# RWKV steps of a hybrid block: outputs in the state's own PSUM bank, a third set of operands, U times M made ahead, and later filling

## The chip, the cores and the metric

The kernel runs on one core of one Trainium2 chip. The metric is the time of one execution on the device in microseconds (us), lower is better; the median of several runs is compared. Engines are named as in the profile: PE is TensorE (PEld its weight loads), DVE VectorE, ACT ScalarE, POOL GpSimd, SP the queue that issues the DMAs.

## The reference

Four layers work on 256 latent and 256 context tokens of width 1024. A layer normalises and modulates the tokens, projects them to 67 blocks of 128 columns, and sends these through three token mixers: gated DeltaNet (GDN, 4 heads), RWKV-7 (8 heads of 64) and mLSTM (4 heads). Every mixer runs in both directions, over the context first and then over the latents, starting from the context's final state. Their outputs are projected, gated and summed, and a mixture of 16 experts follows. In the last layer the context's outputs are not needed any more, only its final states.

```python
def rwkv7_scan(inp, S0):                 # state S (heads, 64, 64)
    def step(S, xt):
        r_t, w_t, k_t, v_t, a_t, b_t = xt
        sa = einsum('bhvk,bhk->bhv', S, a_t)
        S = S * w_t + sa[..., None] * b_t + v_t[..., None] * k_t
        return S, einsum('bhvk,bhk->bhv', S, r_t)

for l in range(DEPTH):
    gdn, rwkv, mlstm, gate = split_cols(modulate(rmsnorm(x, g1), *mod) @ w_in[l])
    a, b, m = gdn_branch(gdn), rwkv_branch(rwkv), mlstm_branch(mlstm)
    x = x + mod[2] * merge_branches((a, b, m), gate, w_branch[l], w_out[l])
    x = x + mod[5] * moe_ec(modulate(rmsnorm(x, g2), *mod), ...)
```

## The kernel before

The 512 tokens (context first) stand on the free axis, channels on the partitions. A layer (`layer`) starts with `rms_scale` and a loop over eight channel blocks that scales, modulates and splits them (`split`) into a rounded high part `hh`, written by ACT, and the rest `hl`, subtracted by POOL; both go to TensorE. `w_in(b, t, ...)` projects one block: its weights are loaded and split in the same way (`load_w`, lines 366 and 367), then 24 matmuls follow (`dense`, line 393).

The order of the work is made by a planner that places, on each engine, the ready instruction with the lowest number first; the program sets that number by due times, in units of about a microsecond from the layer's start (`at`, and `z.due`, which also lets the number grow with the matmul work issued). What is placed stays in that order on the engine; each engine's queue is then executed in order. `D_R`, `D_G` and `T_M` are the due distance of two RWKV pairs, that of two GDN heads, and the start of the mLSTM. `FILL` holds the due times of 36 projections that no scan needs soon (24 gate blocks, 4 output gates, 8 mLSTM inputs): they fill TensorE between the steps of the scans and are stored to DRAM (`gates`). `F0` and `F1` say over which part of the layer's due times they are spread.

RWKV works on pairs of heads, four per layer (`rwkv_pair`). A pair has two streams of tokens, the context (st = 0) and the latents (st = 1), each with both directions. A unit (`rwkv_units`) is one pair and stream: `rwkv_prep` makes the scaled operands AR and BK from decay and keys; `rwkv_unit` multiplies them to the triangles M1, transposes BK and the values (BKt, UV) and stores the triangles to DRAM (`tri_load`). `tri_inverse` inverts the 64x64 triangles of both units at once: small diagonal blocks by substitution on VectorE (lines 428 and 429), then products on TensorE. `rwkv_steps` walks four chunks in each direction. It first makes F, the product of M1 and the values (pf, copied at line 956). A step then multiplies the state X with AR (into bank pu, and, for the outputs, into another bank py), adds F to get R (line 988), multiplies with the inverse, copies the result into UV (lines 994 and 995), and multiplies that with BKt for the next state (lines 1017 and 1018) and with M1 for the outputs, which line 1010 or 1012 reads. After the steps the tail of the pair normalises the outputs and multiplies them by a gate made from R["sgd"] (lines 788 to 808).

PSUM has eight banks: one each for `dm` and `df` (projections) and `ad`, two `ai` (RWKV, mLSTM: `psm`), one `ac` (`psc`), two `bi` (GDN). M1, UV, BKt, AR and two small scale tiles have two buffers, BK one. After RWKV's last tail its SBUF pool is given to the mLSTM; `gdn(3)` is issued there. At the end of the mLSTM line 1448 normalises it, and the branches are merged.

Of the kernel before, what the change touches and what calls it, by code (L numbers as in the profile page):

```python
# [79 lines left out]
BLK = 11.5  # L80
CH = 2
DT = BLK / 8 * 1.0
D_R, D_G, T_M = 160.0, 210.0, 660.0
T1 = 5
P_R, P_G, P_M = D_R * 2.6 / 240, D_G * 3.5 / 170, 8.0
SH = 0.0
# [8 lines left out]


FILL = _fill()
F0, F1 = 0.0, 1.0
SVB = 1
PL = 1  # L100
OFF, PS = 0.0, 1.0
# [52 lines left out]
def tile_backbone(ctx: ExitStack, tc: tile.TileContext, A, out, dbg=None, depth=DEPTH):  # L154
# [319 lines left out]
    def layer(l, P, last, ahead):  # L474
# [14 lines left out]
        gates = dp.tile([40, 128, 512], F32, tag="gates", name=nm("gates"))  # L489
        part = dp.tile([8, 128, 512], F32, tag="part", name=nm("part"))  # L490

        def gated(i, db, ab, th, f):
# [42 lines left out]
                    sy.dma_start(dbg["mg"][:, db, :], acc)  # L535
            return mh, ml

        with scope("gdn", "bi", "bi", 3) as zg:
            with scope("rwkv", "ai", "ac", 3) as zr:

                xT = X["sb"]
                r = rms_scale(zr, X["ss"], 0, "sgd")
                if l > 0:
                    X["dram"] = dp.tile([128, 8, 512], F32, tag="xd", name=nm("xd"))
                    sy.dma_start(X["dram"], xT)
# [1 line left out]
                for k in range(8):  # L547
                    t = zr.mt([512], "t2")
                    ve.tensor_tensor(t, xT[:, k, :], r, ALU.mult)
                    for s in range(2):  # L550
                        ts_ = t[:, s * 256:(s + 1) * 256]
                        ve.tensor_scalar(ts_, ts_, der[:, 0, k, s:s + 1], mod[:, k, s:s + 1], ALU.mult, ALU.add)
                    split(hh[:, k, :], hl[:, k, :], t, gp)

                clock["base"] = tc.cur_priority + 100000

# [13 lines left out]

                at(0)
                G = small_gates(zg, l, P, hh, hl)
                R = rwkv_begin(zr, l, P, w_in, oc)
                pair = [rwkv_inputs(zr, l, 0, P, R, w_in, oc)]
                S = {}

# [129 lines left out]
        return G  # L706


    def rwkv_begin(z, l, P, w_in, oc):
# [23 lines left out]
        thw, adm, sgd = z.mt([512], "thw"), z.mt([512], "adm"), z.mt([512], "sgd")  # L733
        ps = w_in(B_RW, 0)
        shift_mix(ps, 12, thw)
        se.activation(thw, thw, AF.Tanh)
        ps = w_in(B_RA, 0)
        shift_mix(ps, 13, adm)
        ps = w_in(B_RG, 0, oc)
        shift_mix(ps, 14, sgd, oc)  # L740
        se.activation(sgd[:, oc:], sgd[:, oc:], AF.Tanh, scale=0.5)
        ve.tensor_scalar(sgd[:, oc:], sgd[:, oc:], 0.5, 0.5, ALU.mult, ALU.add)
        hb = z.mt([4, 8], "hb")
        ve.tensor_scalar(hb[:, 0, :], P["w0"], 0.5, None, ALU.mult)
        ve.tensor_scalar(hb[:, 1, :], P["a0"], 0.5, None, ALU.mult)
# [3 lines left out]
        return dict(shift_mix=shift_mix, thw=thw, adm=adm, sgd=sgd, hb=hb, ws=ws)  # L749

    def rwkv_inputs(z, l, b, P, R, w_in, oc):

# [11 lines left out]
    def rwkv_units(z, l, b, P, R, pair, units, last, oc, sts=(0, 1)):  # L764

        for st in sts:
            noy = last and st == 0
            z.due(D_R * (b - (0.3, 0.15)[st]), P_R * PS)
            units[b, st] = rwkv_unit(z, b, st, pair[b]["vb"], noy, rwkv_prep(z, b, st, P, R, pair[b], noy, oc))

    def rwkv_pair(z, l, b, P, R, pair, units, dst, last, oc):
# [4 lines left out]
        z.due(D_R * b, P_R * PS)  # L776
        un = [units.pop((b, st)) for st in range(2)]
        inv = tri_inverse(z, 2, lambda g, p, q: un[g]["M1"][64 * p:64 * p + 64, p, q // 4, q % 4, 0:64])
        S = None
        for st in range(2):  # L780
            z.due(D_R * (b + 0.5 + 0.25 * st), P_R * PS)
            S = rwkv_steps(z, st, un[st], inv[st], Y, S, last and st == 0)
            if b < 3 and st == 0:
                rwkv_units(z, l, b + 1, P, R, pair, units, last, oc, (0,))
        z.due(D_R * (b + 1), P_R * PS)

        n = slice(oc, 512)
# [27 lines left out]

    def rwkv_prep(z, b, st, P, R, pr, noy, oc):
# [18 lines left out]
        scl = z.mt([2, 4], "scl", 2)  # L835
        er0 = z.mt([2], "er0", 2)

        def c4(t):
            return t.rearrange("p (c w) -> p c w", c=4)
# [103 lines left out]
    def rwkv_steps(z, st, un, inv, Y, S, noy):  # L943
# [4 lines left out]

        def c4(t):
            return t.rearrange("p (c w) -> p c w", c=4)  # L950
        pf = z.psm()
        for q in range(8):
            for p in range(2):
                hp, vp = slice(64 * p, 64 * p + 64), slice(64 - 64 * p, 128 - 64 * p)
                z.mm(pf[hp, q * 64:q * 64 + 64], M1[vp, p, q // 4, q % 4, 0:64], UV[vp, q // 4, q % 4, p, :], start=True, stop=True)
        ve.tensor_copy(F, pf.rearrange("q (s w) -> q s w", s=8))
        Fv = F.rearrange("p (d s) w -> p d s w", d=2)

        X = None
# [1 line left out]
            X = z.mt([2, 64], "X", 3)  # L961
            ve.tensor_tensor(X, S, er0[:, :, None].to_broadcast([128, 2, 64]), ALU.mult)
        for s in range(4):
            pu = z.psc()
            rhs = Fv[:, :, s, :]
            if X is not None:
                for d in range(2):
                    for p in range(2):
                        hp = slice(64 * p, 64 * p + 64)
                        z.mm(pu[hp, d * 64:d * 64 + 64], AR[hp, d, ch(d, s), 0, :], X[hp, d, :], start=True, stop=True)  # L970


            lo_first = s < 2
            po = None
            if not noy:
                py = z.psm()

                def po(d, hp):
                    sl = d if lo_first else 1 - d
                    return py[hp, sl * 64:sl * 64 + 64]  # L980
                if X is not None:
                    for d in range(2):
                        for p in range(2):
                            hp = slice(64 * p, 64 * p + 64)
                            z.mm(po(d, hp), X[hp, d, :], AR[hp, d, ch(d, s), 1, :], start=d == 0, stop=False, skip_group_check=True)
            if X is not None:
                rhs = z.mt([2, 64], "R", 2)
                ve.tensor_tensor(rhs, pu[:, 0:128].rearrange("p (d w) -> p d w", d=2), Fv[:, :, s, :], ALU.add)
            for d in range(2):
                for p in range(2):  # L990
                    hp = slice(64 * p, 64 * p + 64)
                    z.mm(pu[hp, 256 + d * 64:320 + d * 64], U[hp, d * 4 + s, :], rhs[hp, d, :], start=True, stop=True)
            puv = pu[:, 256:384].rearrange("p (d w) -> p d w", d=2)
            ve.tensor_copy(UV[0:64, :, s, 0, :], puv[0:64])
            ve.tensor_copy(UV[64:128, :, s, 1, :], puv[64:128])
            for d in range(2):
                q = d * 4 + s
                for p in range(2):
                    hp = slice(64 * p, 64 * p + 64)
                    z.mm(pu[hp, 128 + d * 64:192 + d * 64], BKt[:, q, 64 * p:64 * p + 64], UV[:, d, s, p, :], start=True, stop=True)  # L1000
            if not noy:
                for d in range(2):
                    for p in range(2):
                        hp = slice(64 * p, 64 * p + 64)
                        z.mm(po(d, hp), UV[:, d, s, p, :], M1[:, p, d, s, 64:128], start=X is None and d == 0, stop=True, skip_group_check=True)
                a, e = min(s, 3 - s), max(s, 3 - s)
                yv = c4(Y[:, tk])[:, a::(e - a), :][:, 0:2, :]
                pyv = py[:, 0:128].rearrange("p (d w) -> p d w", d=2)
# [752 lines left out]
```

## Time and profile before

| | |
|---|---|
| median of 3 runs | 5061.66 us (5058.88 to 5065.56) |
| the profiled execution's own time | 5072.66 us |
| its span | 5070.9 us |
| mean granted TensorE clock | 0.937 of full speed |
| busy: PE, PEld, DVE | 4530.9, 2946.4, 3067.7 us |
| busy: ACT, POOL | 1417.9, 1432.1 us |

The span reaches from the first to the last instruction; the execution's own time is 1.8 us more. Busy time of PE is modelled, since matmuls are pipelined, and the clock counts beside it. The second layer, from which most rows come, runs from about 1330 to 2620: its first stretch to 1460, the middle to 2114, the end of the scans to 2240, the merge to 2340, and the experts.

### The profile page before, as it was taken

How to read it: one execution, taken by the hardware profiler on the slowest of the kernel's cores; microseconds unless marked ns; L12 is line 12 of the kernel's file. 1: busy time of each engine (PE TensorE's matmuls, PEld its weight loads, DVE VectorE, ACT ScalarE, POOL GpSimd, SP SyncE). 2: the span in 40 equal slices, each digit the busy share in tenths (PEclk: the TensorE clock that was granted, in tenths of full speed). 3: DMA queues.
4: the chain of work that ended last, by engine and by line, in shares of the span. 5: the costliest groups of instructions: out<-in, count | busy, mean ns of one | idle time of the engine just before them, and what ended most of it. 6: DMA issues, size and time to landing. Idle time of an engine off the chain costs nothing. (4 is left out here: it accounts for less than half of the span.)

```text
span 5070.9 us, 84827 instructions
## 1 busy us (share of the span) xinstructions
PE 4530.9 (89%) x31882; PEld 2946.4 (58%) x31882; DVE 3067.7 (60%) x8291; ACT 1417.9 (28%) x2748; POOL 1432.1 (28%) x1831
## 2 busy tenths in 40 slices
PE   7999999899899989889989998998998898887698
PEld 4666666653366666666336666665633666765533
DVE  4777666733477786573337777657433778766422
ACT  3332322220243333222014333322311433321211
POOL 3332332320243242223014334222300534431400
PEclk9999998899999999989999999997999999887899
DMA  5444444579632434346973243443698223322598
GB/s 187 133 125 138 129 143 155 180 264 394 235 109 79 135 99 139 110 157 252 393 271 114 85 125 101 128 115 129 229 387 306 84 84 92 95 77 77 194 389 316
DMA packets 681131, 881.45 MB, mean 174 GB/s; under 512 B 336752, under 2 KB 360304, under 8 KB 667920
## 3 DMA queue, kind: packets, MB, share of 16 engines
q1 hardware_dynamic: 680720, 876.02, 51.5%
q8 instruction: 252, 4.13, 0.3%
q14 instruction: 159, 1.30, 0.1%
HBM read 792.14 MB, written 83.71 MB: 173 GB/s over the span
## 5 line engine op out<-in xcount | busy, mean ns | idle before, releaser
L367 POOL TENSOR_TENSOR wlo<-wraw,whi 128x512 fp32r<-128x512 f32 x696 | 943.5, 1360 | 1969.4 <-ACT whi L366 1806.5
L393 PE MATMUL df<-big,whi 128*128 128x512 f32 (+1 forms) x2944 | 897.0, 385 | 1.7 <-POOL big L367 1.7
L393 PE MATMUL dm<-big,whi 128*128 128x512 f32 (+1 forms) x2368 | 732.1, 388 | 0.0
L366 ACT CAST whi<-wraw 128x512 fp32r<-128x512 f32 x696 | 426.0, 617 | 1045.4 <-PE df L393 528.3
L393 PE MATMUL df<-big,wlo 128*128 128x512 f32 (+1 forms) x1536 | 648.3, 422 | 54.8 <-ACT gt L565 13.5
L393 PEld LDWEIGHTS df<-big,whi 128*128 128x128 f32 x2944 | 564.2, 200 | 97.0 <-issue 6.5
L393 PE MATMUL dm<-big,wlo 128*128 128x512 f32 (+1 forms) x1248 | 521.2, 418 | 46.9 <-POOL wlo L367 13.4
L393 PEld LDWEIGHTS dm<-big,whi 128*128 128x128 f32 x2368 | 453.9, 196 | 80.6 <-issue 1.6
L393 PEld LDWEIGHTS df<-big,wlo 128*128 128x128 f32 x1536 | 304.1, 198 | 187.8 <-issue 86.2
L393 PEld LDWEIGHTS dm<-big,wlo 128*128 128x128 f32 x1248 | 244.7, 196 | 136.8 <-issue 49.9
L1647 PE MATMUL df<-mw,big 128*64 128x512 f32 x1024 | 302.2, 610 | 0.0
L1034 DVE SCALAR_TENSOR_TENSOR cv<-cv,par,cv 128x189 f32<-128x189 f32 (+3 forms) x472 | 243.2, 527 | 38.3 <-ACT cv L1031 33.8
L1694 DVE SCALAR_TENSOR_TENSOR big<-bi,der,big 128x256 f32<-128x256 f32 x448 | 191.8, 479 | 119.7 <-PE bi L1691 119.3
L1647 PE MATMUL dm<-mw,big 128*64 128x512 f32 x1024 | 255.6, 594 | 2.2 <-DMA mw<-in_w_dram 2.1
L1654 POOL MEMSET mada<- 128x512 f32 x32 | 16.8, 524 | 799.8 <-PE bi L1691 350.4
L722 DVE SCALAR_TENSOR_TENSOR big<-cv,muc,big 128x255 f32<-128x255 f32 (+2 forms) x280 | 158.1, 587 | 27.1 <-ACT big L719 24.8
L1647 PEld LDWEIGHTS dm<-mw,big 128*64 128x64 f32 x1024 | 80.8, 137 | 152.4 <-issue 137.0
L211 PE MATMUL ai<-AR,BK 64*128 64x128 f32 (+1 forms) x1024 | 104.6, 311 | 62.0 <-DVE BK L895 32.2
L1685 DVE SCALAR_TENSOR_TENSOR mlof<-ac,aff,mhif 128x512 fp32r<-128x512 f32 x32 | 24.0, 750 | 212.3 <-ACT mhif L1684 212.3
L1681 PE MATMUL ac<-mw,mrawf 128*64 128x512 f32 x512 | 139.6, 600 | 9.9 <-ACT mrawf L1675 9.9
L211 PEld LDWEIGHTS ai<-AR,BK 64*128 64x128 f32 x1024 | 85.9, 207 | 96.0 <-issue 33.2
L308 PE MATMUL ad<-adaw,cs 128*32 128x512 f32 x768 | 116.5, 659 | 26.2 <-DMA adaw<-in_ada_w_dram 21.4
(515 smaller groups left out, 7938.0 us busy)
## 6 DMA issues: line engine op xcount, KB each, us to landing
mw<-in_w_dram SPq DMA_DIRECT2D x768, 512.0 KB, 10.2
wraw<-in_w_in_dram SPq DMA_DIRECT2D x536, 256.0 KB, 2.8
adaw<-in_ada_w_dram SPq DMA_DIRECT2D x96, 1024.0 KB, 5.9
gates<-gt SPq DMA_DIRECT2D x114, 256.0 KB, 3.1
wraw<-in_w_branch_dram SPq DMA_DIRECT2D x96, 256.0 KB, 2.9
t<-gates SPq DMA_DIRECT2D x73, 256.0 KB, 3.5
TU<-zoai SPq DMA_DIRECT2D x128, 128.0 KB, 3.4
wraw<-in_w_out_dram SPq DMA_DIRECT2D x64, 256.0 KB, 5.4
```

Of the source, the lines that this page charges most:

```text
L211: mm(o, a, b, **kw)
L308: mm(ps[32 * j:32 * j + 32, :], cs[:, k, :], wt[:, j, :], start=(k == 0), stop=(k == 7), tile_position=(0, 32 * j))
L366: se.copy(dst_hi, src)
L367: eng.tensor_tensor(dst_lo, src, dst_hi.bitcast(F32), ALU.subtract)
L393: mm(ps[:, c0:c1], a[:, k % 4, :], bk[:, c0:c1], start=(n == 0), stop=(n == 3 * nk - 1))
L722: ve.scalar_tensor_tensor(dst, src, muc[:, 1 + q, rb:rb + 1], dst, ALU.mult, ALU.add)
L1034: ve.scalar_tensor_tensor(dst, src, cw[:, cb, t:t + 1], dst, ALU.mult, ALU.add)
L1647: mm(ps[64 * q:64 * q + 64, :], xe[k // 4][:, k % 4, e0 + q, :], wt[q][:, k2 * 512:(k2 + 1) * 512], start=(k == 0), stop=(k == 7))
L1654: gp.memset(Ow, 0.0)
L1681: mm(py[hf][64 * q:64 * q + 64, :], hT[:, kk, 64 * q:64 * q + 64], wt[q][:, hf * 512:(hf + 1) * 512], start=(kk == 0), stop=(kk == 3))
L1685: ve.scalar_tensor_tensor(yl[hf], py[hf], aff, yh[hf].bitcast(F32), ALU.mult, ALU.subtract)
L1694: ve.scalar_tensor_tensor(xT[:, db, cs_], pcb[:, cs_], der[:, 3, db, s:s + 1], xT[:, db, cs_], ALU.mult, ALU.add)
```

## The change

Eight edits, all within the mixers of a layer:

- A step's outputs lie in columns 384 to 511 of the bank pu (`ac`) that also holds its other three results, in place of a bank of `ai`. Only the first matmul into each half of the partitions starts the bank. The X products for the outputs are issued before R is added. The copy of the upper half of UV, and the output read of the first two steps, go from VectorE to ScalarE.
- AR and the two scale tiles have three buffers.
- F is made for both streams right behind the inverse, in place of at the head of each stream's steps.
- The second unit of the next pair is issued ahead of the pair's tail, and is due 0.1 of a pair earlier, as the first is. The steps are due at 0.4 and 0.55 of a pair in place of 0.5 and 0.75.
- The gate input `sgd` is stored to DRAM and loaded by each tail; its SBUF tile goes. `rms_scale` uses another tile.
- GDN has two scratch buffers `t2` in place of three.
- D_G is 195 for 210, T_M 650 for 660, and the filling is due from 0.1 of the time on.
- The split of hh and hl alternates between POOL and VectorE.

```diff
-D_R, D_G, T_M = 160.0, 210.0, 660.0
+D_R, D_G, T_M = 160.0, 195.0, 650.0
-F0, F1 = 0.0, 1.0
+F0, F1 = 0.1, 1.0
...
-        with scope("gdn", "bi", "bi", 3) as zg:
+        with scope("gdn", "bi", "bi", 2) as zg:
-                r = rms_scale(zr, X["ss"], 0, "sgd")
+                r = rms_scale(zr, X["ss"], 0, "adm")
-                    split(hh[:, k, :], hl[:, k, :], t, gp)
+                    split(hh[:, k, :], hl[:, k, :], t, (gp, ve)[k % 2])
...
+        sy.dma_start(sgdd[:, oc:], sgd[:, oc:])
...
-            z.due(D_R * (b - (0.3, 0.15)[st]), P_R * PS)
+            z.due(D_R * (b - (0.4, 0.25)[st]), P_R * PS)
...
         inv = tri_inverse(z, 2, ...)
+        for (F, _, _), u in zip(inv, un):
+            pf = z.psm()
+            for q in range(8):
+                for p in range(2):
+                    ...
+                    z.mm(pf[hp, q * 64:q * 64 + 64], u["M1"][vp, p, q // 4, q % 4, 0:64], u["UV"][vp, q // 4, q % 4, p, :], start=True, stop=True)
+            ve.tensor_copy(F, pf.rearrange("q (s w) -> q s w", s=8))
         for st in range(2):
-            z.due(D_R * (b + 0.5 + 0.25 * st), P_R * PS)
+            z.due(D_R * (b + 0.4 + 0.15 * st), P_R * PS)
             S = rwkv_steps(z, st, un[st], inv[st], Y, S, last and st == 0)
             if b < 3 and st == 0:
                 rwkv_units(z, l, b + 1, P, R, pair, units, last, oc, (0,))
+        if b < 3:
+            rwkv_units(z, l, b + 1, P, R, pair, units, last, oc, (1,))
         z.due(D_R * (b + 1), P_R * PS)
...
-        z.mm(pgt[:, n], gup, R["sgd"][:, n], start=True, stop=True)
         av = z.mt([512], "t2")
+        sy.dma_start(av[:, n], R["sgd"][:, n])
+        z.mm(pgt[:, n], gup, av[:, n], start=True, stop=True)
...
-        if b < 3:
-            rwkv_units(z, l, b + 1, P, R, pair, units, last, oc, (1,))
...
-        AR, BK = z.mt([2, 4, 2, 64], "AR", 2), z.mt([2, 4, 2, 64], "BK")
+        AR, BK = z.mt([2, 4, 2, 64], "AR", 3), z.mt([2, 4, 2, 64], "BK")
...
+            def mm1(o, p, a, b):
+                z.mm(o, a, b, start=p not in begun, stop=True, skip_group_check=True)
+                begun.add(p)
...
+            def po(d, hp):
+                sl = d if lo_first else 1 - d
+                return pu[hp, 384 + sl * 64:448 + sl * 64]
...
             ve.tensor_copy(UV[0:64, :, s, 0, :], puv[0:64])
-            ve.tensor_copy(UV[64:128, :, s, 1, :], puv[64:128])
+            se.copy(UV[64:128, :, s, 1, :], puv[64:128])
...
                 if lo_first:
-                    ve.tensor_copy(yv, pyv)
+                    se.copy(yv, pyv)
                 else:
                     ve.tensor_tensor(yv, yv, pyv, ALU.add)
```

## Rows read from the trace of the kernel before

**Rows 1.** Windows: span, busy time of each engine (instructions), PEclk, DMA share, GB/s.
```profile
1460.00:2114.00 654.00, 605.47 (x5519) 434.87 (x5517) 460.46 (x1317) 209.30 (x414) 210.23 (x318) 0.96 0.38 111
2114.00:2240.00 126.00, 101.68 (x534) 72.87 (x534) 94.67 (x301) 30.56 (x61) 26.91 (x29) 0.77 0.42 135
840.00:955.00 115.00, 95.83 (x460) 69.16 (x461) 88.84 (x274) 28.09 (x56) 23.61 (x23) 0.74 0.39 128
3404.00:3530.00 126.00, 101.47 (x536) 72.85 (x537) 95.60 (x302) 30.60 (x60) 27.30 (x29) 0.78 0.40 134
4030.00:4605.00 575.00, 489.63 (x5003) 394.33 (x5002) 425.67 (x1233) 190.19 (x399) 211.41 (x320) 0.90 0.31 83
4605.00:4705.00 100.00, 75.31 (x425) 55.00 (x426) 69.44 (x229) 19.47 (x46) 18.20 (x24) 0.67 0.33 97
```

**Rows 2.** Single lines from 1990 to 2260 us: durations, first and last start, forms.
```profile
L808 DVE TENSOR_TENSOR t<-ai,t x1: 678/678/678, 2116.4 to 2116.4; 128x512 f32<-128x512 f32 x1
L1220 DVE TENSOR_TENSOR Ds<-TU x8: 274/286/289, 2017.3 to 2172.7; 64x128 f32<-64x128 f32 x8
L1448 DVE TENSOR_TENSOR mH<-mH,mrr x4: 684/685/694, 2232.0 to 2233.9; 128x512 f32<-128x512 f32 x4
```

**Rows 3.** Line 565, the filling blocks' read, from 2030 to 2130 us.
```profile
L565 ACT ACTIVATE gt<-df x7: 578/590/604, 2039.9 to 2124.4; 128x512 f32<-128x512 f32 x7
```

**Rows 4.** Timeline of the second layer's second RWKV pair: start, duration, instruction.
```profile
1685.22 1.27 SPq L404 DMA_DIRECT2D ziai<-M  x2
...
1764.63 0.28 DVE L1018 TENSOR_TENSOR X<-X,scl 128x128 f32<-128x128 f32 x1
...
1787.81 0.69 DVE L956 COPY TU<-ai 128x512 f32<-128x512 f32 x1 [0.28 <-PE ai L211]
...
1808.80 0.28 DVE L1018 TENSOR_TENSOR X<-X,scl 128x128 f32<-128x128 f32 x1
...
1823.21 0.68 DVE L808 TENSOR_TENSOR t<-ai,t 128x512 f32<-128x512 f32 x1
...
1835.48 0.19 ACT L863 ACTIVATE er<-t 128x4 f32<-128x4 f32 x1
...
1847.55 1.29 SPq L404 DMA_DIRECT2D ziai<-M  x2
```

**Rows 5.** Timeline of one step of that pair, and line 995 from 1330 to 2250.
```profile
1757.34 0.40 PE L211 MATMUL ai<-M,UV 128*64 128x64 f32 x8
1757.56 0.29 DVE L1017 TENSOR_TENSOR X<-ac,X 128x128 f32<-128x128 f32 x1 [1.00 <-PE ac L211]
...
1757.80 0.29 DVE L1012 TENSOR_TENSOR big<-big,ai 128x128 f32<-128x128 f32 x1
...
1758.00 1.30 DVE L1018 TENSOR_TENSOR X<-X,scl 128x128 f32<-128x128 f32 x1
...
1759.93 0.40 PE L211 MATMUL ai<-AR,X 64*64 64x64 f32 x8
1760.14 0.29 DVE L988 TENSOR_TENSOR R<-ac,TU 128x128 f32<-128x128 f32 x1 [0.33 <-PE ac L211]
...
L995 DVE COPY UV<-ac x32: 294/295/296, 1530.9 to 2102.1; 64x128 f32<-64x128 f32 x32
```

**Rows 6.** Timeline of a unit's value copies, both out of one PSUM bank.
```profile
1690.12 0.42 DVE L938 COPY UV<-ai 64x256 f32<-64x256 f32 x1
1690.57 0.37 ACT L937 COPY UV<-ai 64x256 f32<-64x256 f32 x1 [0.98 <-DVE UV L938]
1691.17 0.41 DVE L938 COPY UV<-ai 64x256 f32<-64x256 f32 x1
```

**Rows 7.** Groups of the layer's first split: busy us, mean ns, idle before, releasers.
```profile
L367 POOL TENSOR_TENSOR big<-t,big 128x512 fp32r<-128x512 f32 x8 | 11.6, 1464 | 12.0 <-ACT big L366 12.0
...
L549 DVE TENSOR_TENSOR t<-big,sgd 128x512 f32<-128x512 f32 x8 | 8.6, 1083 | 5.1 <-POOL big L367 3.5 <-ACT sgd L362 1.6
```

**Rows 8.** Waits of ACT from 1460 to 2114 us: total, times, longest.
```profile
ACT whi L366 <- PE df L393: 119.1, 36, 9.0
```

More of the change, by code (lines that the diff above doesn't have):

```diff
@@ L488, in layer @@
         spill = [dp.tile([128, 4, 512], F32, tag=f"br{i}", name=nm("br")) for i in range(2)]
-        gates = dp.tile([40, 128, 512], F32, tag="gates", name=nm("gates"))
+        gates = dp.tile([41, 128, 512], F32, tag="gates", name=nm("gates"))
         part = dp.tile([8, 128, 512], F32, tag="part", name=nm("part"))
@@ L572, in layer @@
                 G = small_gates(zg, l, P, hh, hl)
-                R = rwkv_begin(zr, l, P, w_in, oc)
+                R = rwkv_begin(zr, l, P, w_in, oc, gates[40])
                 pair = [rwkv_inputs(zr, l, 0, P, R, w_in, oc)]
@@ L706, in small_gates, with rwkv_begin @@
         return G
-    def rwkv_begin(z, l, P, w_in, oc):
+    def rwkv_begin(z, l, P, w_in, oc, sgdd):
         muc = z.mt([5, 15], "muc")
@@ L731, in shift_mix @@
             tap(3, o[:, 256:448], p[:, 320:512])
-        thw, adm, sgd = z.mt([512], "thw"), z.mt([512], "adm"), z.mt([512], "sgd")
+        thw, adm, sgd = z.mt([512], "thw"), z.mt([512], "adm"), z.mt([512], "t2")
         ps = w_in(B_RW, 0)
@@ L748, in rwkv_begin @@
         ws = big()
-        return dict(shift_mix=shift_mix, thw=thw, adm=adm, sgd=sgd, hb=hb, ws=ws)
+        return dict(shift_mix=shift_mix, thw=thw, adm=adm, sgd=sgdd, hb=hb, ws=ws)
     def rwkv_inputs(z, l, b, P, R, w_in, oc):
@@ L778, in rwkv_pair @@
         inv = tri_inverse(z, 2, lambda g, p, q: un[g]["M1"][64 * p:64 * p + 64, p, q // 4, q % 4, 0:64])
+        for (F, _, _), u in zip(inv, un):
+            pf = z.psm()
+            for q in range(8):
+                for p in range(2):
+                    hp, vp = slice(64 * p, 64 * p + 64), slice(64 - 64 * p, 128 - 64 * p)
+                    z.mm(pf[hp, q * 64:q * 64 + 64], u["M1"][vp, p, q // 4, q % 4, 0:64], u["UV"][vp, q // 4, q % 4, p, :], start=True, stop=True)
+            ve.tensor_copy(F, pf.rearrange("q (s w) -> q s w", s=8))
         S = None
         for st in range(2):
-            z.due(D_R * (b + 0.5 + 0.25 * st), P_R * PS)
+            z.due(D_R * (b + 0.4 + 0.15 * st), P_R * PS)
             S = rwkv_steps(z, st, un[st], inv[st], Y, S, last and st == 0)
@@ L833, in rwkv_prep @@
         tk = slice(t0, t0 + 256)
-        AR, BK = z.mt([2, 4, 2, 64], "AR", 2), z.mt([2, 4, 2, 64], "BK")
-        scl = z.mt([2, 4], "scl", 2)
-        er0 = z.mt([2], "er0", 2)
+        AR, BK = z.mt([2, 4, 2, 64], "AR", 3), z.mt([2, 4, 2, 64], "BK")
+        scl = z.mt([2, 4], "scl", 3)
+        er0 = z.mt([2], "er0", 3)
         def c4(t):
@@ L950, in c4 @@
             return t.rearrange("p (c w) -> p c w", c=4)
[L951 to L956, printed above, removed]
         Fv = F.rearrange("p (d s) w -> p d s w", d=2)
@@ L963, in rwkv_steps @@
         for s in range(4):
-            pu = z.psc()
+            pu, begun = z.psc(), set()
+            def mm1(o, p, a, b):
+                z.mm(o, a, b, start=p not in begun, stop=True, skip_group_check=True)
+                begun.add(p)
+            lo_first = s < 2
+            def po(d, hp):
+                sl = d if lo_first else 1 - d
+                return pu[hp, 384 + sl * 64:448 + sl * 64]
             rhs = Fv[:, :, s, :]
@@ L969, in rwkv_steps @@
                         hp = slice(64 * p, 64 * p + 64)
[L970 to L981, printed above, removed]
+                        mm1(pu[hp, d * 64:d * 64 + 64], p, AR[hp, d, ch(d, s), 0, :], X[hp, d, :])
+                if not noy:
                     for d in range(2):
@@ L984, in rwkv_steps @@
                             hp = slice(64 * p, 64 * p + 64)
-                            z.mm(po(d, hp), X[hp, d, :], AR[hp, d, ch(d, s), 1, :], start=d == 0, stop=False, skip_group_check=True)
-            if X is not None:
+                            mm1(po(d, hp), p, X[hp, d, :], AR[hp, d, ch(d, s), 1, :])
                 rhs = z.mt([2, 64], "R", 2)
@@ L991, in rwkv_steps @@
                     hp = slice(64 * p, 64 * p + 64)
-                    z.mm(pu[hp, 256 + d * 64:320 + d * 64], U[hp, d * 4 + s, :], rhs[hp, d, :], start=True, stop=True)
+                    mm1(pu[hp, 256 + d * 64:320 + d * 64], p, U[hp, d * 4 + s, :], rhs[hp, d, :])
             puv = pu[:, 256:384].rearrange("p (d w) -> p d w", d=2)
             ve.tensor_copy(UV[0:64, :, s, 0, :], puv[0:64])
-            ve.tensor_copy(UV[64:128, :, s, 1, :], puv[64:128])
+            se.copy(UV[64:128, :, s, 1, :], puv[64:128])
             for d in range(2):
@@ L999, in rwkv_steps @@
                     hp = slice(64 * p, 64 * p + 64)
-                    z.mm(pu[hp, 128 + d * 64:192 + d * 64], BKt[:, q, 64 * p:64 * p + 64], UV[:, d, s, p, :], start=True, stop=True)
+                    mm1(pu[hp, 128 + d * 64:192 + d * 64], p, BKt[:, q, 64 * p:64 * p + 64], UV[:, d, s, p, :])
             if not noy:
@@ L1004, in rwkv_steps @@
                         hp = slice(64 * p, 64 * p + 64)
-                        z.mm(po(d, hp), UV[:, d, s, p, :], M1[:, p, d, s, 64:128], start=X is None and d == 0, stop=True, skip_group_check=True)
+                        mm1(po(d, hp), p, UV[:, d, s, p, :], M1[:, p, d, s, 64:128])
                 a, e = min(s, 3 - s), max(s, 3 - s)
                 yv = c4(Y[:, tk])[:, a::(e - a), :][:, 0:2, :]
-                pyv = py[:, 0:128].rearrange("p (d w) -> p d w", d=2)
+                pyv = pu[:, 384:512].rearrange("p (d w) -> p d w", d=2)
                 if lo_first:
-                    ve.tensor_copy(yv, pyv)
+                    se.copy(yv, pyv)
                 else:
```

## The prediction

> **What bounds the kernel now.** I read the windows by stage first, then the ends of the three scans, then one RWKV pair and one step in the timeline. The reader should look at one thing in the windows: TensorE does not run equally well everywhere. Multiply its busy time by the granted clock and one has its work in full-clock microseconds. In the second layer's long middle stretch that is 605.47 x 0.96 / 654 = 0.889 of the span; in the 126 us before the branches are merged it is 101.68 x 0.77 / 126 = 0.62, the clock having fallen to between its two levels of 1.2 and 2.4 GHz while the engine was less busy. The same dip stands at the same place in the other layers, and the last layer, with half the filling, is thin throughout (489.63 x 0.90 / 575 = 0.766) [rows 1].
>
> What runs in that dip is shown by the ends of the scans. RWKV's last output is multiplied at 2116.4, the mLSTM follows it (its tiles take RWKV's place in SBUF) and is normalised from 2232.0, and GDN's last state product is at 2172.7 [rows 2]. So the layer ends RWKV, then mLSTM, and the mLSTM waits on VectorE step by step while little else is left for TensorE: the last seven of the 36 filling blocks of this layer come out between 2039.9 and 2124.4 [rows 3]. Blocks whose due times lie 28 apart come out about 14 apart there, (2124.4 - 2039.9) / 6, so a due time is a priority and not a gate.
>
> If each dip ran at the middle stretch's rate, its work would take 95.83 x 0.74 / 0.889 = 80 us of 115 (first layer), 88 of 126 (second), 101.47 x 0.78 / 0.889 = 89 of 126 (third), and by the last layer's own rate 75.31 x 0.67 / 0.766 = 66 of 100: 35 + 38 + 37 + 34 = 144 us in four layers. From 2232.0 to 2240 only the mLSTM's own end is left, which nothing can cover; I take these 8 us off in each layer. That leaves 112 us, and it needs the mLSTM to be done about 30 us earlier in each layer.
>
> **Does the change bring the chain 30 us forward?** One RWKV pair, from the store of its triangles to that of the next, takes 162 us (1685.2 to 1847.6) [rows 4]. The first stream's last state is ready at 1764.9 but the second stream's U-times-M product is copied only by 1788.5: the next pair's first unit, due at 0.7 of a pair, went ahead of the second stream, due at 0.75. The new due times (0.6 against 0.55) and the product made ahead turn that round; up to 23.6 us. The pair's own tail, 14.8 us (to 1823.9), stands before the next pair's second unit; moving the unit ahead of it takes the tail off this path. The unit's preparation, 11.8 us to its last exponential at 1835.7, can run during the steps with a third set of operands; its products and the store, another 11.9 us, cannot, since they need the two-deep triangles and the transposed operands that the steps hold. Together up to 50 us per pair, three times per layer. The low bound is zero: the prepared work is not gone, VectorE is busy 460.46 of 654 us, and it may stretch the steps by what it used to take between them. Ten us per pair are enough; nearest to the rows, with about 30% of VectorE free, I take half, 25.
>
> The product itself, 16 matmuls and a copy per stream, is moved and stays as dear. It now stands in front of the first step for both streams, so the first stream now waits for the second's as well: a copy of 0.69 us [rows 4] and sixteen products, at four (eight instructions) in 0.40 us [rows 5] 1.6 us, so 2.3 us, which I count inside the half that I take.
>
> **What a step pays.** All its results now share one bank. In the step shown the state add (1757.56) began before the output products ended (1757.34 + 0.40), and the R add (1760.14) before the X products (1759.93 + 0.40) [rows 5]. If accesses to a bank are put in order, R waits 0.19 us more, and the state add 0.18 and then the output read. Where VectorE does that read, the products' end, the read and the add (1757.74 + 0.29 + 0.29) put the scaling at 1758.32 in place of 1758.00: 0.32 us. Where ScalarE does it, the hand-over counts: VectorE and ScalarE reading one bank took turns, from 1690.54 to 1690.57 and from 1690.94 to 1691.17, so 0.03 and 0.23 us [rows 6], and the add moves from 1757.56 to 1757.74 + 0.03 + 0.29 + 0.23 = 1758.29: up to 0.73. The second of the two UV copies, 0.295 us [rows 5], runs beside the first and is saved, or, if it too takes its turn, costs 0.23. A step therefore pays from 0.19 + 0.32 - 0.30 = 0.2 to 0.19 + 0.73 + 0.23 = 1.2 us, 2 to 9 us in the eight steps of a pair. I take 5; the chain has that to spare, so nothing enters the sum. That VectorE and ScalarE took turns in rows 6 was on the same 64 partitions. The Trainium skill, "PSUM — Partial Sum Buffer", section "PSUM bank collisions raise a hardware error", asks that two engines never touch one bank in the same 32 partitions at once, reads included, and lets different groups of 32 go together. By it the two UV copies, on opposite halves, need no turn, but the ScalarE output read, on all partitions, does: it speaks against putting the outputs there, and by it the price is 0.19 + 0.73 - 0.30 = 0.6 us in the early steps; the sum would be the same.
>
> **The first split.** GpSimd subtracts eight times, 11.6 us, and VectorE waits 3.5 us for it [rows 7]. Four go to VectorE, where a pass over 512 columns took 0.69 us (the copy in rows 4), 2.8 us. The gain is between 3.5 - 2.8 = 0.7 and half of GpSimd's 11.6, 5.8 us; I take 3 per layer, 12 in all.
>
> **Parts at nothing.** Filling due 100 later: TensorE's total is the same, and by rows 3 a free engine takes a block before its time; RWKV's first inputs go ahead of the first blocks, which I count as nothing for want of a row. GDN's earlier due times and its two instead of three scratch buffers: GDN's last product is 59 us before the normalisation, 2232.0 - 2172.7 [rows 2], and a scratch buffer more to wait for costs a store's landing per head. Storing the gate input and loading it four times per layer goes through SP's queue; the load stands in the pair's tail, no longer on the path, except after the last pair, where it may add a few us ahead of the mLSTM; that comes out of the 25. What would be queued behind a late load are SP's weight loads.
>
> **The sum.** 5072.66 - 112 - 12 = 4949 us for an execution like the profiled one. The median of the runs is 11 us under it, so 4938: I say 4940. Its own range, if only half or half as much again of the dips is won, is 4880 to 5000.
>
> **Rivals.** *GDN becomes the end.* The compressed RWKV takes its turns on VectorE. If GDN ends 30 to 40 us later, its 59 us are nearly used, and I give 10 us per layer: 5072.66 - 40 - 12 - 11 = 5010. For it: VectorE's 70%. Against it: GDN's own due times move forward. Chance 0.13.
>
> *TensorE is not the bound even in the middle.* Then the chain sets everything, up to where GDN ends: four times 59 us, 236, and 12: 5072.66 - 236 - 12 - 11 = 4814. For it: weight loads fill only 434.87 of 654 us there [rows 1]. Against it: matmuls are busy 605.47. Chance 0.07. The Trainium skill, "Perfetto Trace Analysis", section "Identifying the Most-Contended Engine", says that matmul busy time is a poor measure of how near TensorE is to its limit and names the share of weight loads; by that rule this rival would be the likeliest.
>
> *ScalarE holds up the steps: slower.* It executes in order, and two copies now stand in its queue on the state's path, twelve instructions per pair. Its casts of weights waited 119.1 us for matmuls, 36 times, 3.3 us each and 9.0 at worst [rows 8]. If each of the twelve stands 4.2 us behind such a cast, the pair's 50 us are gone, and with 9 us for hand-overs a pair is 9 longer; three pairs in four layers are 108, less the 12 of the split: 5062 + 96 = 5158. It decides from about (50 - 9) / 12 = 3.4 us each. Against it: a cast ahead of the copy can only wait for a matmul that TensorE does before it, and between steps that is a few matmuls. Chance 0.12.
>
> *It does nothing.* The order is made from due times; the chain may shorten and the other work spread into the hole: 5062, chance 0.06.
>
> **Chances and range.** The forecast has 0.62; 0.2% (10 us) is about what a measurement of this kernel can tell from no change. Faster: 0.62 + 0.13 + 0.07 = 0.82; same 0.06; slower 0.12. From 4850 to 5040 the range takes in the forecast, the GDN case and a little of the case beyond: about 0.78 together, with the GDN case's upper part at the edge.
>
> **What would show it.** The distance between two stores of RWKV triangles falls from 162 to 120-150 us; RWKV's last output comes 50 us or more earlier within its layer; the stretch before the merge has a clock above 0.9; the first GpSimd subtractions are four. A step takes up to 1 us longer from one state to the next. Wrong: the mLSTM starts as late as before; or it starts earlier and the dip only moves; or ScalarE's UV copy starts some us after its products.

## The result and the profile after

The changed kernel takes 4999.8 us in the median of four runs (4980.37 to 5006.14); the kernel before, beside it, 5063.61 (5058.88 to 5079.16). The medians lie 64 us apart; the comparison of the runs gives a ratio of 0.9848 (95% interval 0.9826 to 0.9871), which is 77 us of 5063.61. Below, versions are compared by such ratios. The forecast was 124 us, with 4999.8 inside its range, though nearer to the 5010 of the rival "GDN becomes the end" than to 4940. The profiled execution took 5006.14 us, with a span of 5004.4 and a mean granted clock of 0.948 (0.937 before).

Windows of the second layer of the changed kernel: from 100 us into the layer to the mLSTM's start, from there to its normalisation, from there to the mixture of experts.

```profile
1424.10:2047.20 623.10, 581.62 (x5389) 416.38 (x5386) 439.40 (x1293) 213.94 (x448) 196.76 (x311) 0.96 0.38 111
2047.20:2157.70 110.50, 100.62 (x574) 73.53 (x572) 87.05 (x264) 32.01 (x63) 30.88 (x30) 0.94 0.38 123
2157.70:2301.90 144.20, 131.23 (x590) 98.66 (x590) 61.02 (x103) 38.03 (x66) 60.66 (x47) 0.99 0.70 237
```

The dip is nearly gone: in the second row TensorE's work at full clock is 100.62 x 0.94 / 110.5 = 0.86 of the span, where [rows 1] gave 0.62 at a clock of 0.77. The last layer's dip is not, see below. But the third stretch, the merge, is now 144.2 us long; before it was 114.7 (880.4 to 995.1 after the layer's start). Its density is 131.23 x 0.99 / 144.2 = 0.90, so it is long because it holds more work. Single lines of the same layer show which.

```profile
L819 DVE TENSOR_TENSOR t<-ai,t x1: 692/692/692, 2035.3 to 2035.3; 128x512 f32<-128x512 f32 x1
L1223 DVE TENSOR_TENSOR Ds<-TU x8: 274/289/994, 1955.0 to 2095.5; 64x128 f32<-64x128 f32 x8
L1451 DVE TENSOR_TENSOR mH<-mH,mrr x4: 680/680/1702, 2157.7 to 2160.5; 128x512 f32<-128x512 f32 x4
L565 ACT ACTIVATE gt<-df x17: 577/592/602, 1942.4 to 2157.4; 128x512 f32<-128x512 f32 x17
L497 DVE SCALAR_TENSOR_TENSOR mg<-mg,df x8: 687/689/689, 2164.8 to 2193.2; 128x512 f32<-128x512 f32 x8
```

Counted from the first scaling of its tokens (line 549), this layer starts at 1324.1, that of before at 1351.6 ("about 1330" above was rough). Against [rows 2], RWKV's last output is at 711.2 after the layer's start in place of 764.8, GDN's last one at 771.4 in place of 821.1, and the normalisation at 833.6 in place of 880.4: 47 to 54 us earlier. GDN still ends 62 us ahead of the normalisation, so it has not become the end. The filling, which ended at 772.8 [rows 3], now ends at 833.3, so it covers the mLSTM. The eight blocks of RWKV's projected branch (the last line), which before stood in the dip, from 796.3 to 857.3 after the layer's start, now come behind the mLSTM, from 840.7 to 869.1. Of 47 us at the normalisation 17 are left where the mixture of experts begins (977.8 against 995.1).

Timeline of the second pair and its steps.

```profile
1621.38 1.26 SPq L404 DMA_DIRECT2D ziai<-M  x2
...
1687.56 0.69 DVE L786 COPY TU<-ai 128x512 f32<-128x512 f32 x1 [0.24 <-PE ai L211]
...
1689.17 0.27 DVE L997 COPY UV<-ac 64x128 f32<-64x128 f32 x1
1689.48 0.26 ACT L998 COPY UV<-ac 64x128 f32<-64x128 f32 x1 [10.34 <-DVE UV L997]
...
1691.70 0.27 ACT L1013 COPY big<-ac 128x128 f32<-128x128 f32 x1 [1.96 <-PE ac L211]
...
1691.99 0.29 DVE L1023 TENSOR_TENSOR X<-ac,scl 128x128 f32<-128x128 f32 x1 [1.81 <-ACT big L1013]
...
1694.85 0.28 DVE L997 COPY UV<-ac 64x128 f32<-64x128 f32 x1 [0.75 <-PE ac L211]
...
1695.18 0.26 ACT L998 COPY UV<-ac 64x128 f32<-64x128 f32 x1
...
1729.74 1.38 SPq L404 DMA_DIRECT2D ziai<-M  x2
...
1758.73 1.35 SPq L404 DMA_DIRECT2D ziai<-M  x2
```

From store to store this pair takes 137 us in place of 162 [rows 4]; the pairs before and after it went from 217 to 187 and from 157 to 152. The next pair's first unit is stored in mid-pair (1729.74). A step, however, is longer: from one state to the next inside a stream 7.7 us in the median of this layer's 24 distances against 5.9. The state's scaling at 1691.99 starts 0.02 us behind ScalarE's output read, and ScalarE's UV copy 0.05 us behind VectorE's.

The first split of the second layer, single lines:

```profile
L549 DVE TENSOR_TENSOR t<-big,adm x8: 684/689/693, 1324.1 to 1337.2; 128x512 f32<-128x512 f32 x8
...
L367 POOL TENSOR_TENSOR big<-t,big x4: 1297/1650/1666, 1326.7 to 1340.9; 128x512 fp32r<-128x512 f32 x4
L367 DVE TENSOR_TENSOR big<-t,big x4: 684/962/1771, 1329.0 to 1341.5; 128x512 fp32r<-128x512 f32 x4
```

Four subtractions each, as forecast. They did not get cheap: VectorE's took up to 1771 ns, and GpSimd's mean over its four is 1566 ns against 1464 over eight [rows 7].

### The profile page after: what moved, and what is told of

The parts are those of the page before. It is cut to its first block, busy times and chain, and to the rows that moved or that the text cites. A ratio compares the mean times of both kernels' runs of the same rounds, so it can differ in the third digit from the quotient of the medians.

```text
span 5004.4 us, 84862 instructions
## 1 busy us (share of the span) xinstructions
PE 4513.4 (90%) x31882; PEld 2934.2 (59%) x31882; DVE 2998.8 (60%) x8123; ACT 1470.0 (29%) x2932; POOL 1405.1 (28%) x1815
## 4 chain that ended last, share of the span: by engine, by line
PE 50%; DVE 20%; DMA 6%; issue 4%; ACT 3%; POOL 2%; SPq 0%; DVEq 0%; ACTq 0%; POOLq 0%
PE df L393 9%; PE dm L393 8%; PE df L1650 5%; PE ai L211 5%; PE bi L211 5%; PE dm L1650 4%; PE bi L1694 3%; PE ac L211 2%; PE ac L1684 2%; PE bi L1684 2%; DMA t<-gates 2%; DVE cv L1037 2%; DMA mw<-in_w_dram 1%; DVE sv L428 1%; POOL wlo L367 1%
## 5 line engine op out<-in xcount | busy, mean ns | idle before, releaser
L1037 DVE SCALAR_TENSOR_TENSOR cv<-cv,par,cv 128x255 f32<-128x255 f32 (+3 forms) x472 | 249.0, 539 | 42.6 <-ACT cv L1034 38.8
L722 DVE SCALAR_TENSOR_TENSOR big<-cv,muc,big 128x252 f32<-128x252 f32 (+2 forms) x280 | 156.6, 581 | 33.2 <-ACT big L719 31.8
L211 PE MATMUL ai<-AR,BK 64*128 64x128 f32 (+1 forms) x1024 | 124.0, 320 | 29.8 <-POOL BK L905 12.3
L1694 PEld LDWEIGHTS bi<-mada,mhif 128*128 128x128 f32 x256 | 48.0, 187 | 155.1 <-issue 82.7
L1684 PE MATMUL bi<-mw,mrawf 128*64 128x512 f32 x512 | 138.1, 592 | 0.0
```

The costliest lines, as they stand in the source:

```text
L211: mm(o, a, b, **kw)
L1037: ve.scalar_tensor_tensor(dst, src, cw[:, cb, t:t + 1], dst, ALU.mult, ALU.add)
L1684: mm(py[hf][64 * q:64 * q + 64, :], hT[:, kk, 64 * q:64 * q + 64], wt[q][:, hf * 512:(hf + 1) * 512], start=(kk == 0), stop=(kk == 3))
L1694: mm(pcb[:, n], y[db // 4][:, db % 4 * 128:(db % 4 + 1) * 128], Cm[:, n], start=y is yh, stop=y is yl)
```

## The experiments

Each ratio is that to the kernel before, run beside it, with its 95% interval. The names in the headings are those under which the versions appear below.

### e1_fill_later

Kernel before, with only the filling's due times changed.

```diff
-F0, F1 = 0.0, 1.0
+F0, F1 = 0.1, 1.0
```

> The kernel before with one constant changed: the filling is due from 0.1 of the layer on. Chain theory (the gain comes from RWKV ending earlier): mLSTM starts where it did, 5050 to 5065 us. Filling theory (the gain comes from keeping filling blocks for the end of the scans): the stretch before the merge fills by itself, 5000 to 5030 us, and the last of the 36 blocks is read after 2140 us in the second layer in place of 2124.

Measured: 5101.91 us, 1.0078 (1.0063 to 1.0093), slower. No theory had that. From the mLSTM's start to its normalisation, in the second layer of the kernel before and then of e1:

```profile
2129.30:2232.10 102.80, 81.98 (x440) 60.24 (x438) 78.92 (x265) 22.30 (x44) 19.62 (x20) 0.75 0.42 133
2129.90:2237.00 107.10, 88.19 (x486) 65.21 (x486) 83.67 (x266) 25.06 (x50) 25.58 (x24) 0.84 0.46 142
```

So later filling does fill a part of the dip: TensorE's work is 88.19 x 0.84 / 107.1 = 0.69 of the span in place of 0.60, and the last block is read 799 us after the layer's start in place of 773. But the work is missing elsewhere. By the sums explained behind the experiments, the dips of four layers lose 37 us less (128 against 165) and the stretches before them some 45 us more (450 against 405). The mLSTM's normalisation came 3 to 4 us later in the first two layers and 10 us earlier in the third, and the last layer became 25 us longer (895.2 against 870.1 to the mixture of experts). What falls is the idea that later filling alone brings a gain.

### e2_order_only

Kernel before with RWKV's new order alone: units earlier and ahead of the tail, three operand buffers, the gate input in DRAM and two GDN scratch buffers (which make the room), U times M behind the inverse. Step, banks, GDN and mLSTM due times, filling and split are as before.

> The kernel before with only the RWKV order of the change: units due earlier, the second unit ahead of the pair's tail, three operand buffers (with the gate input in DRAM and two GDN scratch buffers, which make the room), U times M behind the inverse, steps due at 0.4 and 0.55. Steps, bank, filling, first split and the GDN and mLSTM due times are as before. Chain theory: 5005 to 5030 us, mLSTM starts 40 us or more earlier within its layer. Filling theory: 5045 to 5065 us, although the mLSTM starts earlier.

Measured: 5054.9 us, 0.9981 (0.9967 to 0.9995): about 10 us, inside the range of the filling theory, although by e1 later filling brings nothing by itself. RWKV's last output did come 18 to 24 us earlier in the first three layers, but GDN ended 7 to 13 us later, and the mLSTM took 114 to 119 us from its start to its normalisation in place of 103 to 111 there.

Part of GDN's delay may come from the scratch buffer that was taken away. A GDN head squares its keys and its queries into one such buffer each, and TensorE sums the squares' columns. The second layer's second head, in the kernel before:

```profile
1618.73 0.63 ACT L1076 ACTIVATE t<-KQ 128x512 f32<-128x512 f32 x1
...
1621.67 0.64 ACT L1077 ACTIVATE t<-KQ 128x512 f32<-128x512 f32 x1 [2.31 <-DVE ss L1227]
...
1627.34 2.69 PE L211 MATMUL bi<-cst,t 128*128 128x1 f32 x16
```

and in e2:

```profile
1626.07 0.63 ACT L1079 ACTIVATE t<-KQ 128x512 f32<-128x512 f32 x1 [1.96 <-DVE ss L1230]
...
1638.83 1.86 PE L211 MATMUL bi<-cst,t 128*128 128x1 f32 x8
...
1640.79 0.63 ACT L1080 ACTIVATE t<-KQ 128x512 f32<-128x512 f32 x1 [11.11 <-PE bi L211]
```

With three buffers both squares stand ahead of the sixteen sums. With two, the second square waits until the first one's sums are done, and ScalarE stands still for 11 us. In the last three heads of this layer the second square starts 7 to 15 us after the first in e2 and 3 to 4 us before. All versions with the new order have this wait, and none has the third buffer back, so its price is not known.

### e3_fill_at_0 and e4_own_bank

The changed kernel with `F0 = 0.0`, and the changed kernel with the steps of before (outputs in their own bank, all copies on VectorE).

> The changed kernel with the filling due from 0 again. Chain theory: 4990 to 5015 us, as the change. Filling theory: the dip before the merge is back, 5035 to 5060 us.

> The changed kernel with the steps of before: outputs in a bank of their own and the two copies on VectorE. If the shared bank's hand-overs only eat slack of the chain: 4985 to 5015 us, with steps of 5 us in place of 7. If the slower steps cost time: 4960 to 4985 us. If the bank of ai that the change frees is what lets the next units run beside the steps: 5020 to 5045 us.

Measured: 4965.22 us, 0.9803 (0.9790 to 0.9815), faster than either theory had it, and 5016.42 us, 0.9898 (0.9884 to 0.9913), between the first and the third of its theories. So later filling costs the change some 0.45%, and the new step brings some 0.5%. e3's windows for the same three stretches of the second layer:

```profile
1426.90:2069.80 642.90, 598.53 (x5466) 427.43 (x5466) 453.75 (x1299) 219.26 (x459) 202.25 (x319) 0.96 0.40 113
2069.80:2177.80 108.00, 99.55 (x588) 73.96 (x588) 88.60 (x271) 31.53 (x61) 32.83 (x30) 0.97 0.48 153
2177.80:2296.60 118.80, 111.61 (x506) 84.42 (x506) 55.37 (x97) 33.71 (x59) 51.74 (x40) 0.97 0.71 242
```

With later filling the scan is 20 us shorter here (623.1 against 642.9) and the merge 25 us longer (144.2 against 118.8): TensorE's work was pushed behind the mLSTM. In the last layer nothing comes back at all (860.3 against 840.5 to the mixture of experts).

### f1_pool_split, f2_dve_copies, f3_due_old, f4_split_only

All but the last start from e3. f1: the split on GpSimd alone. f2: the UV copy and the early output read on VectorE, in the shared bank. f3: `D_G`, `T_M` at 210 and 660 again. f4: the kernel before with only the split changed.

```diff
-                    split(hh[:, k, :], hl[:, k, :], t, gp)
+                    split(hh[:, k, :], hl[:, k, :], t, (gp, ve)[k % 2])
```

> The changed kernel with the filling's due times of before (the version that ran at 0.9803 of the kernel before), and the eight subtractions of the first split all on GpSimd again. Theory of the split as the prediction sized it (3 us in each of four layers, 12 us): 0.9827. Rival, the split carries most of what lies between the reordering alone (0.9981) and this version (0.9803), since everything of a layer waits for it: 0.99 or above. Rival, it is worth nothing: 0.9803.

> The version at 0.9803 (changed kernel, filling due as before), with the two copies that the change moved from VectorE to ScalarE (the second UV copy and the early output read) on VectorE again; the outputs stay in the step's own bank. Theory, ScalarE's copies relieve VectorE, which holds up the scan (two copies of 0.29 us in about 24 early and 28 late steps of a layer, 10 to 15 us per layer at most): 0.985 to 0.992. Rival, the gain of the shared bank comes from the freed bank alone, or the hand-over between the two engines eats what the copies save: 0.980. Rival, ScalarE's queue holds up the steps, as the prediction's slower case had it: 0.975 or below.

> The version at 0.9803 (changed kernel, filling due as before), with the GDN heads due every 210 again in place of 195 and the mLSTM at 660 in place of 650. Theory of the prediction, these due times are worth nothing: 0.9803 within 0.002. Rival, the earlier GDN is what lets the faster RWKV count, since the reordering alone ended GDN 7 to 14 us later in each layer: 0.987 or above. Rival, the earlier GDN takes VectorE from RWKV: 0.976 or below.

> The kernel before with only the first split changed: its eight subtractions alternate between GpSimd and VectorE. As the prediction sized it, 12 us: 0.9976; its bounds, 0.7 and 5.8 us per layer: 0.9994 to 0.9954. Rival, a gain at the head of a layer is lost again before the mLSTM, because the order is set anew: 1.000 or above.

Measured: f1 4950.01 us, 0.9756 (0.9734 to 0.9778); f2 4948.17, 0.9759 (0.9738 to 0.9779); f3 5016.09, 0.9892 (0.9873 to 0.9911); f4 5089.91, 1.0036 (1.0023 to 1.0049).

The leading theory failed in all four. f3 and f4 fell where a rival had put them (the earlier GDN lets the faster RWKV count; a gain at the head is lost again), f2 came close to its last rival, and f1 is under all of its values. The split, sized as a gain of 12 us, costs 0.36% in the kernel before and 0.47% in the changed one; the copies on ScalarE cost 0.44% here; and the due times, sized at nothing, are worth 0.9% in the changed kernel. Single lines of f3's second layer (start 1335.2), then e3's (start 1326.9), show the last:

```profile
L1223 DVE TENSOR_TENSOR Ds<-TU x4: 274/282/675, 2147.2 to 2155.0; 64x128 f32<-64x128 f32 x4
...
L1451 DVE TENSOR_TENSOR mH<-mH,mrr x4: 684/684/691, 2200.8 to 2202.6; 128x512 f32<-128x512 f32 x4
```

```profile
L1223 DVE TENSOR_TENSOR Ds<-TU x4: 272/452/700, 2103.3 to 2114.4; 64x128 f32<-64x128 f32 x4
...
L1451 DVE TENSOR_TENSOR mH<-mH,mrr x4: 679/686/1166, 2177.8 to 2180.7; 128x512 f32<-128x512 f32 x4
```

Within its layer GDN ends 32 us later in f3 (819.8 against 787.5) and the normalisation comes 15 us later (865.6 against 850.9), with RWKV's last output only 9 later. GDN still ends 46 us ahead of the normalisation, so it does not have to be the last to cost time. That its last head and the mLSTM use VectorE together is an explanation that is argued, not tested.

### g1_pool_dve, g2_due_only, g3_order_due, g4_due_651

g1: e3 with f1's and f2's edits together. g2: the kernel before with only the two due times changed. g3: e2 with those due times; it differs from g1 in nothing but the outputs' own bank. g4: g1 with `T_M = 651.0`.

```diff
-D_R, D_G, T_M = 160.0, 210.0, 660.0
+D_R, D_G, T_M = 160.0, 195.0, 650.0
```

> The version at 0.9803 (changed kernel, filling due as before) with both edits that made it faster one at a time: the first split on GpSimd alone (0.9756 by itself) and the two PSUM copies on VectorE (0.9759 by itself). Theory, they are two separate costs and add up: 0.971. Rival, both only relieve the same thing, or are no more than another order that fell out well: 0.975 to 0.978.

> The kernel before with only the due times changed: GDN heads every 195 in place of 210, the mLSTM at 650 in place of 660. Theory, GDN's end was not what the mLSTM waited for in the kernel before (it ended 59 us ahead of the normalisation), so earlier GDN only takes VectorE from RWKV: 0.998 to 1.006. Rival, the due times carry a gain of their own (0.9 per cent, as undoing them in the changed kernel cost): 0.991.

> The reordering of RWKV (0.9981 by itself) with the due times of the change (195, 650); the step's two banks, the filling and the first split are as before. It differs from the version with the split on GpSimd and the copies on VectorE, sent along, by nothing but the step's outputs in their own bank. Theory, GDN had become the later end once RWKV was reordered (7 to 14 us later in each layer), so reordering and due times only work together: 0.985 to 0.989, and the shared bank brings the rest to 0.971. Rival, the shared bank is worth nothing: the same time as that version, within 0.2 per cent. Rival, due times count only with the shared bank: 0.995 or above.

> The version with the split on GpSimd and the copies on VectorE, sent along, with the mLSTM's due time at 651 in place of 650: an edit that no theory gives a price. Within 0.2 per cent of that version if the order of the work is stable against a shift of one; 0.3 per cent or more away from it, on either side, if a new order alone moves the time by as much as the smaller differences that these experiments found.

Measured: g1 4936.11 us, 0.9739 (0.9723 to 0.9754); g2 5024.45, 0.9917 (0.9900 to 0.9933); g3 4995.09, 0.9857 (0.9839 to 0.9874); g4 4938.29, 0.9742 (0.9720 to 0.9765).

g1 beats both kernels. Whether the two gains add up, to 0.9712, is not decided: the intervals of the four versions allow it and allow less. With the split on GpSimd, the copies' place is worth 0.17%, inside the intervals. g4 lies on g1, so a shift of one in a due time does not move the median, although in the profiled executions single layers are up to 9 us longer and 4 us shorter. g2, in place of costing time, as its first theory had it, brings 42 us, as its rival said; order and due times together (g3), inside the range of g3's first theory, bring more than their sum (1.43% against 0.19% + 0.83%); the shared bank adds 1.18%. The second layer of g2 (start 1334.2), single lines:

```profile
L808 DVE TENSOR_TENSOR t<-ai,t x1: 681/681/681, 2081.1 to 2081.1; 128x512 f32<-128x512 f32 x1
...
L1220 DVE TENSOR_TENSOR Ds<-TU x4: 273/452/731, 2128.0 to 2133.1; 64x128 f32<-64x128 f32 x4
...
L1448 DVE TENSOR_TENSOR mH<-mH,mrr x4: 684/684/691, 2202.2 to 2204.1; 128x512 f32<-128x512 f32 x4
```

RWKV's code and due times are untouched, yet its last output comes 18 us earlier within the layer (746.9 against 764.8), GDN's 22 and the normalisation 12 (868.0 against 880.4). What else the edit moves: D_G also sets when GDN's inputs are due, and by the slots that these leave free it shifts ten of the 36 filling blocks by 11.5 to 34.5. Which of D_G, T_M and these blocks brings the gain, no run separates.

## Why the prediction came out right, and where it did not

The account below adds up windows of about 12 us over four layers, by stage, for one profiled execution of each version (e2's was 18 us over its median, the others less off): TensorE's idle time, plus its busy time times one minus the granted clock. "Work" is busy time times clock. The stages end 100 us into the layer, at RWKV's last output, at the mLSTM's normalisation, at the mixture of experts, and at the layer's end. The 45 to 47 us ahead of the first layer are in the span alone. From the row of g3 on, each row adds one part to the row above it.

```
us lost in    head  scans  dip  merge  experts   sum   work  span
before          68    336  165     60      121   750   4274  5071
e2 order        68    335  138     65      121   727   4298  5071
g2 due times    68    332  121     60      121   702   4273  5022
g3 both         68    316   89     60      118   651   4290  4990
g1 + bank       67    282   72     59      122   602   4290  4939
f1 + ScalarE    70    284   81     56      121   612   4288  4948
e3 + split      76    297   86     60      121   640   4277  4964
after, + fill   79    306   83     77      122   667   4292  5004
```

**The dip** was the right place. The work is the same to 0.6% in all these rows, so time is lost or won in TensorE's gaps and clock; but 0.6% is 25 us, and smaller differences between rows say little. The dip's loss fell by 82 us where 112 were forecast: 79 in the first three layers, forecast at 86, and 4 in the last, forecast at 26, where it still loses 43 of 47. The scans' loss fell by 30, a term that the sum did not have (the rival "TensorE is not the bound even in the middle" had the place, at several times the size); the other stages lost 29 more. Net 83, less 18 us by which the added-up work differs, is within 2 us of the 66.5 between the two spans.

**The chain** came forward about as forecast: 48, 54 and 50 us in the first three layers ("50 us or more"), 10 in the last, which the forecast counted like the others. **What brought it was not what the prediction named.** The reordering, credited with all of it, is worth 10 us alone, with GDN's scratch buffer taken away beside it. The failed step is "parts at nothing": "GDN's last product is 59 us before the normalisation" was read as slack, and the scratch buffer was priced at a store's landing per head, where it made one square wait for the other's sums, by up to 15 us. Earlier GDN and mLSTM due times are worth 42 us on the kernel before and 63 on the reordered one (0.9981 to 0.9857). The rival "GDN becomes the end" had the direction and, in the first three layers, the size: undoing the due times in e3 costs 9, 11, 5 and 26 us in the four layers, priced at 10 each. Its mechanism, a GDN that ends last, did not come; that the size fits is luck. That the earlier heads leave VectorE free for RWKV's last pairs is argued from g2's lines and not tested further.

**The shared bank** was priced at 2 to 9 us per pair, covered, and no benefit was looked for. It brings about 60 us (g3 to g1: 0.9857 to 0.9739, two kernels that differ in nothing else); in the profiled pair 51, with 34 of loss less in the scans and 17 in the dip. Why is open. RWKV's `ai` products have two banks, and in g3's second layer one of them was held for a step's outputs, from their first product to their read, for 151 us, 4.3 us a step in the median of 32. But this layer gained only 3 us by giving the bank back; 28 of the 51 came in the first layer, 10 in each of the others. TensorE's wait before RWKV's triangle products, 62.0 us before, does not decide it either. It was

```profile
L211 PE MATMUL ai<-AR,BK 64*128 64x128 f32 (+1 forms) x1024 | 108.0, 311 | 43.2 <-POOL BK L905 17.7 <-DVE BK L904 15.7 <-DVE M L930 5.2
```

for g3 (groups of instructions: busy, mean ns, idle before), and for g1

```profile
L211 PE MATMUL ai<-AR,BK 64*128 64x128 f32 (+1 forms) x1024 | 109.5, 301 | 32.9 <-DVE BK L904 19.6 <-POOL BK L905 6.4 <-DVE rr L471 2.7
```

These waits are mostly for the operand BK. Only the one for VectorE's read of M, 5.2 us in g3, is one for a bank. That the freed bank is the cause, rather than the order that follows from it, is therefore argued and not shown.

**What a step pays** came out within its bounds of 0.2 to 1.2 us, as far as it can be told. In the second layer the median step is 6.3 us with both copies on VectorE and 6.7 to 6.8 with them on ScalarE (f2 and g1 against e3 and f1), 0.4 to 0.5 us more; in the first layer it is the other way round (8.1 and 7.6 against 7.2). With the outputs in their own bank and the same order it is 6.5 (g3), so there the shared bank itself made no step longer. The rest of the changed kernel's 7.7 goes with the order and the filling: e3, with earlier filling, has 6.7, and e2, whose steps are those of before, 7.4. ScalarE's UV copy, which the prediction hoped to run beside VectorE's, began after it in all 32 cases of the second layer (0.03 us behind in the median), and its output read overlapped none of the state's adds and scalings in 16 cases. The trace lists ScalarE's wait as one for VectorE's copy, so the program orders the two, which also write one tile. The Trainium skill, "PSUM — Partial Sum Buffer", section "PSUM bank collisions raise a hardware error", lets accesses to different groups of 32 partitions go together; no run here shows it. The slower rival, ScalarE's queue holding up the steps by 3.4 us each, did not come: the longest gap was 1.1 us before a UV copy and 1.2 before an output read.

**The first split** was forecast at 12 us of gain; the term had the wrong sign, by about 24 us (f1 to e3). Its reading of the head was right: the first decay activation comes 31 us into the second layer in place of 35.6, in f4 and e3 alike, and in e3's four layers 10 us earlier in sum. What failed is the step from there to the end: the table shows 6 us more lost in the first 100 us and 13 in the scans. Why the order behind an earlier start is worse was not settled.

**Filling due later**, at nothing by "a free engine takes a block before its time", costs about 23 us here and 0.78% in e1. An engine does so only if the order was placed that way, and work shifted past the last scan stands in the merge. Two readings of it were off: the due times of the seven blocks in [rows 3] lie 11.5 to 23 apart (21 in the mean, not 28), and the first block is due 115 later, the last not at all.

So the forecast was right in sign, place and range by errors that partly cancel. In us of 5063: order and due times 72, bank 60; ScalarE's copies -9 (not told apart from nothing in f1), split -24, filling -23. These are the steps of one chain of versions from the kernel before to the changed one, so their sum has to give the 77 measured (76 by rounding) and is no proof of the parts; in another order of the steps they can have other sizes.

## What to carry to other kernels

When two chains share an in-order engine, the distance between one chain's end and the common end need not be slack: give its due time a run of its own. A scratch buffer taken from a ring makes a later writer wait for other readers, on an in-order engine with all that stands behind it, so look in the trace for what it waits for. A scratch bank held through a recurrence may cost the work behind it in the same ring, so count how long each bank is held before giving one away or sharing one. Give each small part of a combined change its own run: of six parts here two cost time and a third gained nothing, and leaving these three out makes 4936 us of 5000.

## What the runs showed of the hardware

VectorE's four subtractions of that split cost 0.68 and 0.69 us where GpSimd stood still, and 1.77 and 1.24 us where one of GpSimd's ran beside them (timeline of the same layer, beside passes at 1337.55 and 1340.91).

```profile
1337.55 1.44 POOL L367 TENSOR_TENSOR wlo<-wraw,whi 128x512 fp32r<-128x512 f32 x1 [0.42 <-ACT whi L366]
1337.77 1.77 DVE L367 TENSOR_TENSOR big<-t,big 128x512 fp32r<-128x512 f32 x1
```

Over the whole run, VectorE's subtractions of this form took 0.68 to 0.69 us in the 26 cases without a pass of GpSimd beside them (0.1 us of overlap at most) and 0.68 to 1.84 us, 1.13 in the median, in the other 38. So not every one is slowed, but a price of 0.69 us, taken from a copy that ran by itself, was too low for this place.
